# The low parts of a trunk kernel's projection weights: an accumulating transfer in place of VectorE's subtraction

## The chip, the core and the metric

The kernel runs on one core of one Trainium2 chip. The metric is the device time of one execution in microseconds (us). Before the change it is 2383.87 us, the median of three runs (2382.72 to 2384.26).

## What is computed

One inference step of a two-layer hybrid decoder trunk, for 1024 prompt tokens and 8 sample tokens that share all weights, model width 1024, everything in float32. Layer 0 mixes with a gated linear recurrence beside a convolution module, layer 1 with a short gated convolution; each layer ends in a SwiGLU with a hidden width of 2816.

```python
def _even_mixer(x, s0, conf_buf, w_in, w_out, ...):
    p = x @ w_in                                  # 1024 x 3072
    ...                                           # recurrence; depthwise convolution, LayerNorm, swish
    y = jnp.concatenate([o, c], axis=-1) @ w_out  # 1024 x 1024
def _odd_mixer(x, sc_buf, w_in, conv_w, w_out):
    p = x @ w_in                                  # 1024 x 3072
    ...
    return y @ w_out, ...
def _swiglu(x, w1, w3, w2):
    return (jax.nn.silu(x @ w1) * (x @ w3)) @ w2
def _trunk(...):
    for l in range(DEPTH):
        m, ... = _even_mixer(...) if l % 2 == 0 else _odd_mixer(...)
        x = _layernorm(ALPHA * x + m, ln_mix_w[l], ln_mix_b[l])
        x = _layernorm(ALPHA * x + _swiglu(x, ffn_w1[l], ffn_w3[l], ffn_w2[l]), ln_ffn_w[l], ln_ffn_b[l])
```

## The kernel before

The 1032 tokens stand in the columns and are cut into three chunks of 384, 384 and 264 (the last holds the 8 samples). Channels stand on the 128 partitions, in blocks of 128.

TensorE multiplies in a reduced-precision form of float32 (F32R). To keep float32's accuracy every operand is kept as two F32R tiles, a rounded high part and a low part that holds the rest, and every product is three matmuls: low weight by high activation (L141), high weight by low activation (L142), high by high (L143), all into one PSUM bank.

A *unit* is a block of weights for 128 outputs: 128 partitions by up to eight blocks of 128 inputs, 512 KB. `load_unit` (L123) makes one: it takes the tiles `wh` and `wl` (three buffers of each, `W_BUFS`) and `raw` (four buffers, `R_BUFS`), issues the load of `raw` on SyncE's queue (L131), and calls `split` (L119), in which ScalarE writes the high part (L120) and VectorE the low part (L121, `raw` minus `wh`). `mm` (L139) then runs 24 matmuls for a unit of eight input blocks and one chunk (12 for a unit of four). A buffer of `wh` and `wl` becomes free when the last matmul of its unit is done, so a unit can be prepared as soon as the unit three before it has been used up.

The *classic* projections are all that go through `load_unit`: the input and output projections of both mixers (`head_units`, `gate_units`, `conv_units`, `mix1`, `out_proj`), the upper SwiGLU products of the chunks that are not in the fast scheme (`ffn_up`), and the first two lower products of chunk 0 (`ffn_down`, units of four blocks). By the loops there are 281 such units in 282 loads (the first unit comes in two halves): 93 serve chunk 2 alone (20 and 36 in `Swiglu.main`, 6 and 6 in the heads of the two SwiGLUs, 8 and 8 in the output projections, 6 and 3 in `mix1`), 112 serve one chunk of 384, 41 two chunks, 19 three, and 16 are units of four blocks. The rest of the SwiGLU work has its own loads: `Swiglu.down` (load at L612) and `Swiglu.project` (a seven-product scheme over chunks 0 and 1, load at L677). They use the same buffers `wh`, `wl` and `raw`, and call `split` too. So do the activations.

Instructions are traced in program order, with priorities, and a scheduler fixes each engine's order at build time; every engine, and every queue, then runs in that order and waits for semaphores. GpSimd (POOL) has little to do: three transfers and two casts at the start, and the power of minus one half in `rsqrt_small` (L194), once in each of 15 normalisations and 16 times in the recurrence. In a normalisation TensorE broadcasts its result (L239).

Of the kernel before, what the change touches and what calls it, by code (L numbers as in the profile page):

```python
# [19 lines left out]
AF = mybir.ActivationFunctionType  # L20
ALU = mybir.AluOpType
# [47 lines left out]
def trunk(ctx: ExitStack, tc: tile.TileContext, xT, win0, wout0, win1, wout1, w1, w3, w2, vecs, sh, scf, ssc,  # L69
          masks, eye, yT, hp, cp_o, sp_o, hs, cs_o, ss_o):  # L70
    nc = tc.nc
    VE, SC, GP, PE = nc.vector, nc.scalar, nc.gpsimd, nc.tensor
# [46 lines left out]
    def split(hi, lo, src):  # L119
        SC.copy(hi, src)  # L120
        VE.tensor_tensor(lo, src, hi.bitcast(F32), ALU.subtract)  # L121

    def load_unit(src, kt, n=NK):  # L123

        wh = wsp.tile([P, NK, P], F32R, name="wh")
        wl = wsp.tile([P, NK, P], F32R, name="wl")
        raw = wsp.tile([P, NK * P], F32, name="raw", bufs=R_BUFS).rearrange("p (k f) -> p k f", f=P)
        src = src.rearrange("p (k f) -> p k f", f=P)
        for k in range(0, kt, n):
            e = min(k + n, kt)  # L130
            nc.sync.dma_start(raw[:, k:e], src[:, k:e])  # L131
            split(wh[:, k:e], wl[:, k:e], raw[:, k:e])
        return wh, wl, kt

    def mm(unit, c, parts=None):
# [16 lines left out]
    first_x = load_x(0, 2)  # L152
    next(first_x)
    first_unit = [load_unit(win0[4], NK, 4)]
    for _ in first_x:
        pass
# [111 lines left out]
    def out_proj(wsrc, chunks):  # L268

        for m in range(NK):  # L270
            u = load_unit(wsrc[m], NK)
            for c in chunks:
                residual(m, c, mm(u, c), True)

    def ffn_up(tile_of, l, m, chunks, put, table=True):

        sl = {}
        u = load_unit(w1[l, m], NK)
        for c in chunks:
            s = tile_of(CH[c][1] - CH[c][0])  # L280
            ps = mm(u, c)
            if table:
                SC.activation(s, ps, AF.Silu)
            else:
                SC.activation(s, ps, AF.Sigmoid)
                VE.tensor_tensor(s, ps, s, ALU.mult)
            sl[c] = s
        u = load_unit(w3[l, m], NK)
        for c in chunks:
            s = sl[c]  # L290
            VE.tensor_tensor(s, mm(u, c), s, ALU.mult)
            split(*put(m, c), s)
# [656 lines left out]
```

## Time and profile before

| | us |
|---|---|
| median of three runs | 2383.87 |
| the profiled execution | 2385.06 |
| its span, first to last instruction | 2383.2 |
| TensorE busy (matmuls) | 2333.2 |
| VectorE busy | 1701.4 |
| ScalarE busy | 874.2 |
| GpSimd busy | 45.3 |
| mean granted TensorE clock | 0.989 of full speed |

The profiled execution is 1.9 us longer than its span and 1.2 us longer than the median. Busy time counts an engine's own instructions, overlaps once; matmuls overlap each other, so one matmul's own duration is longer than the time by which it moves the next on. A wait is put down to what came last.

### The profile page before, as it was taken

What the parts mean: (1) busy time and instruction counts of PE and PEld (TensorE: products, weight loads), DVE (VectorE), ACT (ScalarE), POOL (GpSimd) and SP (SyncE); (2) the same over time, 40 slices, a digit from 0 to 9 for tenths busy, and PEclk for the clock granted to TensorE, in tenths of its full rate; (3) what the DMA queues carried; (4) which work ended last, traced back from release to release, by engine and by line L of the source; (5) the groups of instructions that cost most, each with busy time, mean ns of one, the idle gap of its engine ahead of it and who ended that gap; (6) DMA issues with size and microseconds to landing.
All of it is one profiled execution on the core that took longest, in us unless ns stands there. A gap on an engine that the chain in (4) does not pass through costs nothing.

```text
span 2383.2 us, 36586 instructions
## 1 busy us (share of the span) xinstructions
PE 2333.2 (98%) x14974; PEld 2293.0 (96%) x14974; DVE 1701.4 (71%) x2943; ACT 874.2 (37%) x1479; POOL 45.3 (2%) x40
## 2 busy tenths in 40 slices
PE   9999999999899999999998999999999999999997
PEld 8999899999899999999998999999999999999997
DVE  8998789897863336777686423667957777777775
ACT  5434353335631223332354211435513332332553
POOL 0000000000000000000000000000000000000000
PEclk9999999999999999999999999999999999999998
DMA  5322222453341221222342311334402222132663
GB/s 186 116 78 73 88 78 77 123 167 113 116 131 45 79 73 48 68 80 71 119 149 88 90 53 45 90 115 142 133 27 71 63 80 68 57 89 80 194 196 98
DMA packets 85560, 229.79 MB, mean 96 GB/s; under 512 B 8225, under 2 KB 26401, under 8 KB 85137
## 3 DMA queue, kind: packets, MB, share of 16 engines
q1 hardware_dynamic: 85232, 227.02, 30.9%
q8 instruction: 117, 1.92, 0.3%
q0 software_dynamic: 160, 0.45, 0.1%
q14 instruction: 51, 0.41, 0.1%
HBM read 220.22 MB, written 7.21 MB: 95 GB/s over the span
## 4 chain that ended last, share of the span: by engine, by line
PE 91%; DVE 4%; ACT 2%; POOL 1%; DMA 1%; issue 1%; SPq 0%; POOLq 0%; DVEq 0%; ACTq 0%
PE mm L141 23%; PE mm L142 23%; PE mm L143 23%; PE mm L692 6%; PE mm L693 6%; PE mm L691 6%; PE sm L335 2%; DVE wl L121 1%; POOL rs L194 1%; PE sm L239 1%; DVE r L216 1%; DVE acc L225 1%; ACT r L254 0%; PE sm L382 0%; ACT wh L120 0%
## 5 line engine op out<-in xcount | busy, mean ns | idle before, releaser
L120 ACT CAST wh<-raw 128x1024 fp32r<-128x1024 f32 (+1 forms) x466 | 468.6, 1007 | 899.4 <-PE mm L143 607.5
L121 DVE TENSOR_TENSOR wl<-raw,wh 128x1024 fp32r<-128x1024 f32 (+1 forms) x466 | 544.1, 1169 | 230.4 <-ACT wh L120 226.5
L141 PE MATMUL mm<-x2h,wl 128*128 128x264 f32 x1216 | 349.7, 288 | 7.0 <-DVE wl L121 6.9
L143 PE MATMUL mm<-x2h,wh 128*128 128x264 f32 x1216 | 346.8, 285 | 0.0
L142 PE MATMUL mm<-x2l,wh 128*128 128x264 f32 x1216 | 346.3, 285 | 0.0
L266 DVE TENSOR_TENSOR r<-r,mm 128x384 f32<-128x384 f32 (+1 forms) x336 | 171.5, 521 | 99.6 <-PE mm L143 99.2
L141 PEld LDWEIGHTS mm<-x2h,wl 128*128 128x128 f32 x1216 | 229.8, 189 | 9.6 <-DVE wl L121 8.3
L142 PEld LDWEIGHTS mm<-x2l,wh 128*128 128x128 f32 x1216 | 230.0, 189 | 1.6 <-issue 0.8
L143 PEld LDWEIGHTS mm<-x2h,wh 128*128 128x128 f32 x1216 | 229.1, 188 | 0.1
L141 PE MATMUL mm<-hb,wl 128*128 128x384 f32 (+1 forms) x672 | 211.4, 320 | 8.4 <-ACT hb L120 4.8
L142 PE MATMUL mm<-hb,wh 128*128 128x384 f32 (+1 forms) x672 | 213.1, 319 | 0.0
L143 PE MATMUL mm<-hb,wh 128*128 128x384 f32 (+1 forms) x672 | 212.8, 318 | 0.0
L482 DVE SCALAR_TENSOR_TENSOR cc<-r,vec,cc 128x256 f32<-128x256 f32 (+17 forms) x360 | 189.7, 561 | 0.9
L141 PEld LDWEIGHTS mm<-hb,wl 128*128 128x128 f32 x672 | 125.9, 190 | 10.7 <-ACT hb L120 7.0
L141 PE MATMUL mm<-x0ha,wl 128*128 128x384 f32 x384 | 132.7, 346 | 1.9 <-DVE wl L121 1.9
L143 PE MATMUL mm<-x0ha,wh 128*128 128x384 f32 x384 | 133.2, 347 | 0.0
L142 PE MATMUL mm<-x0la,wh 128*128 128x384 f32 x384 | 132.3, 345 | 0.8 <-DVE x0la L121 0.8
L143 PE MATMUL mm<-x0hb,wh 128*128 128x384 f32 x384 | 132.0, 344 | 0.0
L141 PE MATMUL mm<-x0hb,wl 128*128 128x384 f32 x384 | 131.3, 342 | 0.0
L142 PE MATMUL mm<-x0lb,wh 128*128 128x384 f32 x384 | 131.0, 341 | 0.0
L143 PE MATMUL mm<-x1hb,wh 128*128 128x384 f32 x384 | 130.8, 341 | 0.0
L142 PE MATMUL mm<-x1lb,wh 128*128 128x384 f32 x384 | 130.5, 340 | 0.0
(310 smaller groups left out, 5242.8 us busy)
## 6 DMA issues: line engine op xcount, KB each, us to landing
raw<-in_w SPq DMA_DIRECT2D x256, 512.0 KB, 3.7
raw<-in_win SPq DMA_DIRECT2D x88, 512.0 KB, 3.7
raw<-in_wout SPq DMA_DIRECT2D x48, 512.0 KB, 3.6
raw<-in_w SPq DMA_DIRECT2D x16, 256.0 KB, 2.7
out_yT<-r SPq DMA_DIRECT2D x8, 384.0 KB, 3.4
S0t<-in_sh SPq DMA_DIRECT2D x8, 256.0 KB, 3.2
out_hs<-S0t SPq DMA_DIRECT2D x8, 256.0 KB, 2.0
r<-in_xT SPq DMA_DIRECT2D x4, 384.0 KB, 7.5
```

The costliest lines, as they stand in the source:

```text
L120: SC.copy(hi, src)
L121: VE.tensor_tensor(lo, src, hi.bitcast(F32), ALU.subtract)
L141: PE.matmul(ps, wl[:, k, :], h, start=k == 0, stop=False)
L142: PE.matmul(ps, wh[:, k, :], l, start=False, stop=False)
L143: PE.matmul(ps, wh[:, k, :], h, start=False, stop=k == kt - 1)
L194: GP.tensor_tensor(dst, dst, mhalf[:p, :n], ALU.pow)
L266: VE.tensor_tensor(v, v, ps, ALU.add)
L335: PE.matmul(ps[:sr, c * 64:(c + 1) * 64].rearrange("p (b i) -> p b i", i=hh), kp[:, c * P:c * P + sr], qr, start=True, stop=True)
L482: VE.scalar_tensor_tensor(acc[:, lo:W], u[:, 30 + lo - d:30 + W - d], col(V_DW + (30 - d) * 4 + i), acc[:, lo:W], ALU.mult, ALU.add)
L691: PE.matmul(ps, w[1][:, k], t[0][:, k], start=k == 0, stop=False)
L692: PE.matmul(ps, w[0][:, k], t[1][:, k], start=False, stop=False)
L693: PE.matmul(ps, w[0][:, k], t[0][:, k], start=False, stop=k == 3)
```

## The change

`load_unit` calls a new function in place of `split`. ScalarE writes the high part as before. Then ScalarE, and no longer VectorE, writes the low tile, with the negated rounded weights. Then GpSimd's queue issues a transfer that reads the same weights from HBM a second time and adds them to what stands in the low tile. The result is the same low part, weights minus high part. `split` stays as it is for the activations, `Swiglu.down` and `Swiglu.project`.

```diff
+    def split_w(hi, lo, raw, src):
+
+        SC.copy(hi, raw)
+        SC.activation(lo, raw, AF.Copy, scale=-1.0)
+        nc.gpsimd.dma_start(lo, src, accum_op=ALU.add)
+
     def load_unit(src, kt, n=NK):
...
             nc.sync.dma_start(raw[:, k:e], src[:, k:e])
-            split(wh[:, k:e], wl[:, k:e], raw[:, k:e])
+            split_w(wh[:, k:e], wl[:, k:e], raw[:, k:e], src[:, k:e])
         return wh, wl, kt
```

## Rows read from the trace of the kernel before

**Rows 1.** The page's first part (busy us, share, instructions), busy tenths in 40 slices.

```profile
PE 2333.2 (98%) x14974; PEld 2293.0 (96%) x14974; DVE 1701.4 (71%) x2943; ACT 874.2 (37%) x1479; POOL 45.3 (2%) x40
...
PE   9999999999899999999998999999999999999997
...
DVE  8998789897863336777686423667957777777775
```

**Rows 2.** The page's chain that ended last, by engine.

```profile
PE 91%; DVE 4%; ACT 2%; POOL 1%; DMA 1%; issue 1%; SPq 0%; POOLq 0%; DVEq 0%; ACTq 0%
```

**Rows 3.** Waits, whole span: who waited for whom: us in total, times, longest.

```profile
ACT wh L120 <- PE mm L143: 607.5, 169, 10.4
...
PE sm L239 <- POOL rs L194: 15.6, 15, 2.1
...
PEld mm L141 <- DVE wl L121: 11.1, 9, 3.8
...
PE mm L141 <- DVE wl L121: 8.9, 7, 3.6
```

**Rows 4.** Instructions on tile raw: duration in ns min/median/max, first and last start.

```profile
L120 ACT CAST wh<-raw x466: 607/1050/1062, 7.3 to 2355.5; 128x1024 fp32r<-128x1024 f32 x140, 128x512 fp32r<-128x512 f32 x16
L121 DVE TENSOR_TENSOR wl<-raw,wh x466: 676/1219/1232, 8.1 to 2356.5; 128x1024 fp32r<-128x1024 f32 x140, 128x512 fp32r<-128x512 f32 x16
L131 SPq DMA_DIRECT2D raw<-in_w x144: 327/328/895, 283.1 to 2340.6; - x144
L131 SPq DMA_DIRECT2D raw<-in_win x90: 327/328/647, 1.2 to 1528.6; - x90
...
L131 SPq DMA_DIRECT2D raw<-in_wout x48: 327/328/340, 186.1 to 1653.9; - x48
```

**Rows 5.** ScalarE by line and shape: busy us, mean ns of one | idle before.

```profile
L120 ACT CAST hb<-hb 128x384 fp32r<-128x384 f32 x56 | 28.7, 512 | 30.5 <-DVE hb L733 30.5
...
L439 ACT ACTIVATE k<-mm 128x384 f32<-128x384 f32 x8 | 3.9, 487 | 0.0
```

**Rows 6.** Timeline of the last stage, three engines: start us, length us, instruction.

```profile
2311.43 1.05 ACT L120 CAST wh<-raw 128x1024 fp32r<-128x1024 f32 x1 [1.82 <-PE mm L143]
...
2312.51 1.23 DVE L121 TENSOR_TENSOR wl<-raw,wh 128x1024 fp32r<-128x1024 f32 x1 [0.65 <-ACT wh L120]
...
2311.24 0.28 PE L141 MATMUL mm<-x2h,wl 128*128 128x264 f32 x1
...
2317.04 0.28 PE L141 MATMUL mm<-x2h,wl 128*128 128x264 f32 x1
```

**Rows 7.** Stretches: their us, then busy us (and instructions) of each engine, clock, DMA.

```profile
2311.20:2331.70 20.50, 20.50 (x172) 20.50 (x171) 11.35 (x15) 9.11 (x13) 0.00 (x0) 1.00 0.58 180
...
1516.50:1537.00 20.50, 20.50 (x120) 20.50 (x119) 14.50 (x24) 12.00 (x24) 0.00 (x0) 1.00 0.38 122
505.00:520.20 15.20, 15.20 (x90) 15.20 (x89) 15.04 (x30) 5.17 (x9) 0.00 (x0) 1.00 0.55 151
1344.00:1513.00 169.00, 169.00 (x1081) 169.00 (x1080) 57.55 (x100) 26.89 (x61) 0.00 (x0) 1.00 0.18 51
```

**Rows 8.** The page's DMA issues: count, KB each, median us from issue to landing.

```profile
raw<-in_w SPq DMA_DIRECT2D x256, 512.0 KB, 3.7
...
raw<-in_w SPq DMA_DIRECT2D x16, 256.0 KB, 2.7
```

**Rows 9.** Timeline of GpSimd: the issue of its largest transfer.

```profile
2.50 0.54 POOL L164 DMA_DIRECT2D mraw<-in_masks  x1
```

**Rows 10.** DMA issues of the first 32 us: count, KB each, us to landing.

```profile
raw<-in_win SPq DMA_DIRECT2D x8, 512.0 KB, 5.9
...
mraw<-in_masks POOLq DMA_DIRECT2D x1, 256.0 KB, 7.2
```

**Rows 11.** The page's DMA queues: packets, MB, time as share of 16 engines' span.

```profile
q1 hardware_dynamic: 85232, 227.02, 30.9%
```

**Rows 12.** Waits of SyncE's queue: us in total, times, longest.

```profile
SPq L131 <- DVE wl L121: 1026.8, 204, 14.4
```

## The prediction

> **What bounds the kernel now.** Read the engines' busy times first: TensorE is busy for 98% of the span, VectorE for 71%, ScalarE for 37% [rows 1]. The chain that ended last says the same: 91% of it is TensorE's, 4% VectorE's [rows 2]. So VectorE's work, though long, is hidden nearly everywhere, even where its slices stand at 8 and 9 tenths (the first 650 us). What VectorE's subtraction costs now is read from the waits: TensorE's matmuls waited 8.9 us for it and its weight loads 11.1 us (two views of mostly the same waits) [rows 3]. That, some 10 to 20 us of 2383, is the most that taking the subtraction away can give directly.
>
> Next, who sets when a unit's low part is made. ScalarE's cast waited 607.5 us, 169 times, for a unit's last matmul [rows 3]: units are not late because ScalarE or VectorE is slow, they are started when one of three buffers comes free. It is a ring of three. The last stage shows one turn: a buffer comes free as a new unit begins at 2311.24, the cast starts at 2311.43, the subtraction runs from 2312.51 to 2313.74, and TensorE needs the unit at 2317.04, two units after the release [rows 6]. 3.3 us are spare. If a unit takes L from release to ready and is used for p, three buffers allow one unit per (L + p)/3, and TensorE is the bound only while L is below two units' time.
>
> The time of a unit is read from stretches in which TensorE never idles [rows 7]: 24 matmuls of 264 columns 2.9 us (20.50 x 24/172), of 384 columns 4.1 us (20.50 x 24/120), 12 of 384 columns 2.0 us (15.20 x 12/90), 72 for three chunks 11.3 us (169 x 72/1081). One such unit's last matmul ends about 0.15 us after the next has begun, so p is 3.05, 4.25 and 2.2.
>
> **What is removed.** 282 of the 466 subtractions, one for each load at L131 (144 + 90 + 48) [rows 4]. 266 are of 1.22 us and 16 units are half as wide, at 0.68: 335 us of VectorE's 1701, nearly all of it beside matmuls. I count back 9 us, the matmuls' own waits.
>
> **What is added on ScalarE.** 282 negations of the raw weights. The cast of the same tile takes 1.05 us, the half one 0.61 [rows 4]. An activation with a factor of -1 takes 0.487 us on 384 columns where the cast takes 0.512 [rows 5], so 1.05 us for 1024 columns, 0.62 for 512. 289 us together bring ScalarE to 1163 us, 49%: no bound, but inside every unit's L.
>
> **What is added on GpSimd and the DMA engines.** 282 accumulating transfers. Nothing in this trace accumulates, so I bound X, the time from the negation's end to the landing. Below, it is a plain 512 KB load from SyncE's queue, 3.7 us [rows 8], plus GpSimd's part of the issue, 0.54 us [rows 9]: 4.3, with a little sharing 4.5. Above, it is GpSimd's only large transfer, 256 KB in 7.2 us among the start's loads [rows 10], plus 1.0 us for twice the bytes (3.7 against 2.7 [rows 8]) and 0.8 for the reading of the sums: 9. What I take is built up: 227.02 MB held 16 engines for 30.9% of the span [rows 11], 736 us, or 1.7 us for 512 KB. To add, an engine must fetch the old content of the low tile too, a second pass over as many bytes: 1.7 more. And the transfer never runs alone. SyncE's next load waits for the buffer `raw` that the subtraction frees, 1026.8 us in 204 waits [rows 12]; now the negation frees it, so load and accumulation start at the same moment and share the engines; I charge a third of the load's 1.7. X = 3.7 + 0.5 + 1.7 + 0.6 = 6.5 us, nearer to the plain load than to the crowded start, as most of the kernel is not crowded. For a half-wide unit 2.7 + 0.5 + 0.85 + 0.3 = 4.35.
>
> The second pass rests on no row. The Trainium skill ("Collectives: The Full Stack", section "The bandwidth ceiling: the fold count and why AG ≠ RS ≠ AR") says that the DMA engines' adder needs two source reads for each piece, and that the reads halve the rate, not the adding. No run here shows it yet. Without that pass X would be 4.8 and the sum below about 50 us instead of 122.
>
> **The sum.** L is now the handover 0.1, cast 1.05, negation 1.05, handover 0.05, X 6.5: 8.75 us, where it was 2.4.
> - The 93 units of chunk 2 alone: (8.75 + 3.05)/3 = 3.93 against 2.9, so 1.03 each: 96 us. The bubble opens before each L141 that starts a unit.
> - The 16 half units: L = 0.1 + 0.62 + 0.62 + 0.05 + 4.35 = 5.74; (5.74 + 2.2)/3 = 2.65 against 2.0: 10 us.
> - The 112 units of one chunk of 384: (8.75 + 4.25)/3 = 4.33 against 4.1. That is 0.23 each, 26 us if all stood back to back, 0 if other matmuls (the recurrence, the norms) always lie between; I take 12.
> - The 60 units of two and three chunks last 7 us and more; two of them cover L wholly: 0.
> - The start: TensorE waits for the first half unit, whose subtraction takes 0.68 [rows 4]. In its place stand 0.62 and a transfer among the start's loads, 4.35 to 7.2: +5.
> - GpSimd's queue: the power of each normalisation (TensorE waits for it 15 times already, 15.6 us [rows 3]) now stands in order behind accumulations that wait for negations, which wait for TensorE to free a buffer. Behind one issue it costs 0.5 each, behind a whole unit 3: 8 to 45 us, I take 8.
> - SyncE's queue keeps its 282 loads in their order; each waits for ScalarE instead of VectorE, at nearly the same time, and there are four `raw` buffers: 0.
> 96 + 10 + 12 + 5 + 8 - 9 = 122 us on an execution of 2385.06, 2507; the median lies 1.2 lower: **2506 us**.
>
> With X = 4.5 the first term is 34 us ((6.75 + 3.05)/3 = 3.27), the second about 5, the third 0, the start 4, the queue 8, less 9: 42, or 2426. With X = 9 it is 174 (4.77 per unit), 25 for the half units, 70 of at most 119 for the third, 8, 8, less 9: 276, or 2660.
>
> **Rivals.**
> *The DMA engines become the bound.* A chunk-2 unit then needs 1.7 for the load and 3.4 for the accumulation, 5.1 us of all engines, more than its 2.9. In `Swiglu.main` one unit in three has no accumulation: (2 x 5.1 + 1.7) - 3 x 2.9 = 3.2 for each of 28 threes, 90 us; the other 37 units 2.2 each, 81; the wide ones up to 1.0 each, I take 80; start, queue and half units 13 more: 264 us, 2648. For it: the DMA share is 0.58 in the last stage already [rows 7]. Against: that share leaves room, and loads can run ahead.
>
> *The transfer is cheap and the kernel gets faster.* The point that decides is L = two units' time, 5.8 us for chunk 2: X = 3.5. Then no ring is late, the start costs 3, and TensorE gets back up to 20 us of waits and something of the norms, where VectorE's queue gets shorter: about 2370. At X = 3.7, the plain load's time, a chunk-2 unit loses 0.1 (9 us in all), start and queue take a few more, and gain and loss cancel: about 2383. Against: GpSimd's one transfer of half the size took 7.2 us, and a SyncE load of 512 KB beside it 5.9 [rows 10]. The Trainium skill ("DMA: Bandwidth & Descriptors", section "Anatomy of one DMA — SWDGE (gpsimd) path") gives a GpSimd transfer a fixed 2.0 us plus its bytes at 436 GB/s, 3.2 us for 512 KB as an estimate: by that rule this rival would come true. The row stands against it: the same rule gives 2.6 us for the 256 KB that took 7.2.
>
> *VectorE was the true bound of the first 650 us* (8 to 9 tenths busy), and its relief by 150 us there shows. Against: TensorE's own slices there stand at 8 and 9 tenths [rows 1], so at most its idle time returns, and that is in the 20 us above. That ScalarE becomes the bound is excluded by its 49%.
>
> **Chances.** The ring with X from 4.5 to about 8: 0.62. The DMA engines as bound, or a dearer transfer: 0.24, of which a little over half ends below 2670. The cheap transfer: 0.10, half of it faster, half the same. Slower than before but below 2420: 0.04. From 2420 to 2670 lie 0.62 + 0.14 = 0.76, near the 8 in 10 that are wanted. A measurement of this kernel tells 0.2%, some 5 us, from no change. Faster 0.05, the same 0.05, slower 0.90.
>
> **What would show it.** Landing times of the accumulations near 6.5 us, and longer than those of the plain loads. VectorE near 1366 us and ScalarE near 1163. TensorE waiting for the landing of `wl` before L141, most of it from 1150 to 1260 and after 2180 us, in bubbles of about 1 us once a unit; almost nothing from 692 to 1148 and 1344 to 1513 us, where units last 7 to 11 us. Stretches of chunk 2 alone going from 2.9 to about 3.9 us a unit. The forecast is wrong if the landings are under 4 us, if the bubbles stand at L239 behind GpSimd's power rather than at L141, or if the wide stages lose as well, which would be the engines' bandwidth.

## The result, and the profile after

The changed kernel takes 2653.34 us (2647.16 to 2659.31), the kernel before 2383.3: a ratio of 1.1133, interval 1.1104 to 1.1163. The forecast was 2506, so the loss is 270 us where 122 was forecast: the sign and the range held, the size did not. The profiled execution has a span of 2648.3 us.

The page of the changed kernel first: busy us of the engines, then the granted clock and the DMA engines' share in 40 slices.

```profile
PE 2411.4 (91%) x14974; PEld 2347.9 (89%) x14974; DVE 1405.6 (53%) x2661; ACT 1130.7 (43%) x1761; POOL 275.9 (10%) x322
...
PEclk8999999999899999999989999988899999999898
DMA  8764666897782551214855644978722221226895
```

Set against [rows 1]: TensorE was idle for 50.0 us (2383.2 - 2333.2) and is idle for 236.9, which is 187 more. And it is busy for 78 us longer with the same 14974 matmuls. 187 + 78 = 265, the whole difference of the spans. VectorE has lost 296 us and nobody gained by it.

What TensorE waits for, from the view of waits (who, for whom: us in total, times, longest):

```profile
POOL wl L127 <- ACT wl L126: 941.4, 181, 53.1
ACT wl L126 <- PE mm L147: 562.4, 208, 12.7
PE mm L147 <- DMA wl<-in_w: 110.0, 56, 10.5
...
PE mm L147 <- DMA wl<-in_wout: 49.5, 19, 10.2
PE mm L147 <- DMA wl<-in_win: 31.6, 14, 10.1
```

L147 is the L141 of before, L126 the negation, L127 the accumulation. The last three lines, 191 us in 89 waits, are the added idle time: TensorE waits for the accumulation to land. They are not the bubbles of about 1 us at each unit that the forecast had as a sign: 51 of the 89 are under 1.5 us, and 16 of over 3 us make 106 of the 191. The second line says why nobody starts it earlier: ScalarE's negation waits for a unit's last matmul with the low weights, as its cast did for the last of all in [rows 3].

The DMA issues (count, KB each, median us from issue to landing) and the two queues (packets, MB, time as a share of 16 engines' span):

```profile
raw<-in_w SPq DMA_DIRECT2D x256, 512.0 KB, 4.9
wl<-in_w POOLq DMA_DIRECT2D x128, 512.0 KB, 7.6
raw<-in_win SPq DMA_DIRECT2D x88, 512.0 KB, 6.5
wl<-in_win POOLq DMA_DIRECT2D x88, 512.0 KB, 7.1
...
wl<-in_wout POOLq DMA_DIRECT2D x48, 512.0 KB, 8.0
```
```profile
q0 software_dynamic: 40768, 143.59, 30.8%
q1 hardware_dynamic: 85232, 227.02, 25.9%
```

The accumulations land after 7.1 to 8.0 us, and the plain loads, 3.7 before [rows 8], now take 4.9 to 6.5. A MB that is added holds the engines for 0.308 x 2648.3 / 143.59 = 5.68 us, a MB on the queue of the loads, which carries the smaller transfers too, for 0.259 x 2648.3 / 227.02 = 3.02.

Where the time goes: stretches with the same work, first of the kernel after, then of the kernel before (stretch, its us, busy us and instructions of PE, PEld, DVE, ACT, POOL, then clock, DMA share, GB/s).

```profile
440.00:602.00 162.00, 146.34 (x883) 137.14 (x881) 95.07 (x218) 80.01 (x135) 33.30 (x39) 0.96 0.88 210
602.00:787.00 185.00, 146.73 (x866) 140.84 (x867) 84.95 (x145) 109.89 (x158) 32.74 (x37) 0.91 0.82 194
787.00:1259.00 472.00, 470.18 (x2906) 469.86 (x2906) 243.95 (x398) 138.00 (x190) 15.34 (x18) 1.00 0.34 89
1259.00:1397.00 138.00, 104.06 (x759) 100.04 (x758) 65.37 (x108) 78.36 (x110) 19.45 (x23) 0.89 0.73 183
...
1483.00:1652.00 169.00, 169.00 (x1080) 169.00 (x1079) 39.18 (x84) 39.82 (x75) 12.81 (x15) 1.00 0.43 99
1652.00:1927.00 275.00, 221.45 (x1276) 213.26 (x1275) 110.98 (x186) 153.02 (x215) 47.27 (x54) 0.90 0.82 192
...
2410.00:2648.00 238.00, 186.38 (x1365) 178.46 (x1363) 88.04 (x150) 116.45 (x153) 32.03 (x37) 0.91 0.76 199
```
```profile
414.00:554.00 140.00, 137.34 (x868) 131.76 (x867) 125.72 (x259) 50.20 (x95) 4.74 (x4) 0.99 0.44 136
554.00:697.00 143.00, 135.99 (x870) 133.49 (x869) 119.89 (x178) 79.30 (x126) 5.23 (x3) 0.98 0.41 126
697.00:1166.00 469.00, 467.93 (x2902) 467.61 (x2902) 265.94 (x417) 122.10 (x173) 0.00 (x0) 1.00 0.22 69
1166.00:1274.00 108.00, 97.61 (x763) 95.16 (x762) 85.63 (x126) 58.91 (x89) 3.91 (x2) 0.95 0.47 143
...
1343.00:1512.00 169.00, 169.00 (x1081) 169.00 (x1080) 58.06 (x101) 26.77 (x60) 0.00 (x0) 1.00 0.18 51
1512.00:1717.00 205.00, 201.34 (x1280) 198.79 (x1279) 156.82 (x225) 102.04 (x161) 4.92 (x3) 0.99 0.42 129
...
2199.00:2383.00 184.00, 169.38 (x1365) 166.17 (x1363) 126.65 (x184) 85.08 (x119) 4.76 (x3) 0.96 0.51 161
```

The stretches of long units lose 3 and 0 us. The last one loses 54, which the forecast had named. But 140 to 162, 143 to 185 and 205 to 275 us are stretches of single chunks of 384 columns for a large part, and the forecast had charged these units with 12 us in all. In the losing stretches the granted clock falls too, from 0.95 to 0.99 down to 0.89 to 0.96.

One turn of the ring shows both. It is from the timeline of 2446 to 2460 us (start us, length us, instruction, idle time before it), ScalarE and GpSimd:

```profile
2447.18 1.06 ACT L126 ACTIVATE wl<-raw 128x1024 fp32r<-128x1024 f32 x1 [1.21 <-PE mm L147]
2448.15 1.03 ACT L125 CAST wh<-raw 128x1024 fp32r<-128x1024 f32 x1
```
```profile
2448.53 0.88 POOL L127 DMA_DIRECT2D wl<-in_w  x1 [17.40 <-ACT wl L126]
```

The low buffer comes free at 2447.18, the negation ends at 2448.24, the transfer is issued at 2448.53, and the matmuls that need it begin at 2457.3, when it has landed. TensorE's last matmul of a unit had ended at 2453.2 and two of a normalisation at 2453.9; from then it was idle for 3.5 us. The negation runs ahead of the cast, here and in 236 of the 282 units, so the cast mostly no longer lies on the path. L, from free to landed, is 10.1 us here. The matmuls that follow, as stretches:

```profile
2457.30:2463.00 5.70, 5.66 (x26) 5.69 (x27) 2.84 (x4) 0.44 (x1) 0.00 (x0) 0.50 1.05 275
2463.00:2469.00 6.00, 6.00 (x48) 5.87 (x47) 2.42 (x4) 5.60 (x9) 1.71 (x2) 0.95 0.74 150
```

After these 3.5 us of waiting the granted clock is 0.50, the level of 1.2 GHz, and 26 matmuls take nearly as long as 48 do next. At the pace of the second stretch they would have taken 3.2 us: the wait costs its own 3.5 us and then 2.5 more behind it.

Matching every unit's first and last matmul in the two traces tells what each kind of unit lost (us; the number of units by this matching; the rest of a unit's loss lies between its ends):

| kind of unit | forecast | measured | of it idle ahead | of it slower matmuls |
|---|---|---|---|---|
| chunk 2 alone (88; the forecast counted 93) | 96 | 134 | 94 | 33 |
| one chunk of 384 (116; the forecast: 112) | 12 | 96 | 79 | 7 |
| half units (16) | 10 | 13 | 6 | 6 |
| two and three chunks (60) | 0 | 20 | 10 | 9 |
| the start | 5 | 10 | 8 | 1 |
| GpSimd's queue, waits given back | -1 | | | |
| units that VectorE still serves (184) | | -8 | 0 | -15 |

The matching sums to 197 us idle, 41 of slower matmuls and 27 between the ends; the page, which counts otherwise, has 187 idle and 78 more busy.

### The profile page after: what moved, and what is told of

Same layout as the page of the kernel before. It is cut to its first block, busy times and chain, and to the rows that moved or that the text cites. A ratio compares the mean times of both kernels' runs of the same rounds, so it can differ in the third digit from the quotient of the medians.

```text
span 2648.3 us, 37279 instructions
## 1 busy us (share of the span) xinstructions
PE 2411.4 (91%) x14974; PEld 2347.9 (89%) x14974; DVE 1405.6 (53%) x2661; ACT 1130.7 (43%) x1761; POOL 275.9 (10%) x322
## 3 DMA queue, kind: packets, MB, share of 16 engines
q0 software_dynamic: 40768, 143.59, 30.8%
q1 hardware_dynamic: 85232, 227.02, 25.9%
## 5 line engine op out<-in xcount | busy, mean ns | idle before, releaser
L126 ACT ACTIVATE wl<-raw 128x1024 fp32r<-128x1024 f32 (+1 forms) x282 | 290.6, 1031 | 563.0 <-PE mm L147 562.4
L147 PE MATMUL mm<-x2h,wl 128*128 128x264 f32 x1216 | 367.8, 303 | 118.8 <-DMA wl<-in_w 78.3
L147 PEld LDWEIGHTS mm<-x2h,wl 128*128 128x128 f32 x1216 | 243.7, 200 | 133.0 <-issue 48.4
L148 PE MATMUL mm<-x2l,wh 128*128 128x264 f32 x1216 | 360.8, 297 | 0.0
L127 POOL DMA_DIRECT2D wl<-in_w x144 | 123.3, 857 | 1482.0 <-DVE wl L121 730.2
L121 DVE TENSOR_TENSOR wl<-raw,wh 128x1024 fp32r<-128x1024 f32 (+1 forms) x184 | 209.6, 1140 | 94.4 <-ACT wh L120 92.0
L147 PE MATMUL mm<-hb,wl 128*128 128x384 f32 (+1 forms) x672 | 211.1, 319 | 3.8 <-ACT hb L120 3.6
L488 DVE SCALAR_TENSOR_TENSOR cc<-r,vec,cc 128x384 f32<-128x384 f32 (+15 forms) x360 | 191.2, 562 | 2.5
L147 PE MATMUL mm<-x1ha,wl 128*128 128x384 f32 x384 | 137.4, 358 | 44.7 <-DMA wl<-in_wout 22.6
L147 PE MATMUL mm<-x0ha,wl 128*128 128x384 f32 x384 | 135.1, 352 | 27.4 <-DMA wl<-in_win 13.1
L270 DVE SCALAR_TENSOR_TENSOR r<-r,mm 128x384 f32<-128x384 f32 (+1 forms) x96 | 48.9, 510 | 165.0 <-PE mm L149 164.6
L149 PE MATMUL mm<-x1ha,wh 128*128 128x384 f32 x384 | 135.5, 353 | 0.0
L148 PE MATMUL mm<-x1la,wh 128*128 128x384 f32 x384 | 134.7, 351 | 0.0
```

What stands on the lines that cost most here:

```text
L126: SC.activation(lo, raw, AF.Copy, scale=-1.0)
L127: nc.gpsimd.dma_start(lo, src, accum_op=ALU.add)
L147: PE.matmul(ps, wl[:, k, :], h, start=k == 0, stop=False)
L148: PE.matmul(ps, wh[:, k, :], l, start=False, stop=False)
L149: PE.matmul(ps, wh[:, k, :], h, start=False, stop=k == kt - 1)
L488: VE.scalar_tensor_tensor(acc[:, lo:W], u[:, 30 + lo - d:30 + W - d], col(V_DW + (30 - d) * 4 + i), acc[:, lo:W], ALU.mult, ALU.add)
```

## The experiments

The kernel each is made from, its edit, the expectation, the result. Ratios are to the kernel before, run beside it. L and the landings are medians from the traces. L is counted there from the start of ScalarE's first step for the low part (the negation; the cast in experiment 3) to the landing, so a late start of that step is not in it.

**1. What ScalarE's second pass costs alone.** From the kernel after; the addition on VectorE:

```diff
-        nc.gpsimd.dma_start(lo, src, accum_op=ALU.add)
+        VE.tensor_tensor(lo, raw, lo.bitcast(F32), ALU.add)
```


> As the changed kernel, but VectorE adds the weights to the negated high part; no accumulating transfer. ScalarE's negation and the new order of ScalarE's work stay. Ring theory (the loss is the transfer's time inside a ring of three buffers): the low part is ready about 2.4 to 3.5 us after a buffer comes free, under the 5.8 us that two chunk-2 units last, so the time is that of before, 2375 to 2395 us. Rival (ScalarE's 290 us more, or the order of work that the scheduler chose, cause the loss): over 2450 us.

2398.61 us, 1.0054 (1.0036 to 1.0073). ScalarE works 1130.2 us as in the kernel after, and the loss is 13 us by the ratio, 15 by the medians, a little more than expected. The transfer in the addition's place accounts for the other 255.

**2. What GpSimd's queue costs alone.** From the kernel before; the classic loads issued by GpSimd:

```diff
-            nc.sync.dma_start(raw[:, k:e], src[:, k:e])
+            nc.gpsimd.dma_start(raw[:, k:e], src[:, k:e])
```


> The kernel before, with the 282 plain loads of the classic units issued by GpSimd instead of SyncE; nothing is added. It shows what a plain transfer of 512 KB from GpSimd's queue costs from issue to landing. By the prediction's terms (3.7 us plain, 0.5 more for GpSimd's issue) 4.2 to 4.5 us, against 5.6 us for the fastest accumulations of the changed kernel: then the adding itself costs 1.1 to 1.4 us. Rival: the queue is what is dear, and the plain loads land after 5.5 us or more too. Time near before, 2383 to 2400 us, as loads run one buffer ahead.

2374.45 us, 0.9959 (0.9945 to 0.9972): a little faster than the kernel before, and the only version here that beats both. A transfer of the same size on the two queues, and GpSimd's queue, from its page:

```profile
q0 software_dynamic: 39616, 143.59, 19.8%
...
raw<-in_w POOLq DMA_DIRECT2D x128, 512.0 KB, 3.9
raw<-in_w SPq DMA_DIRECT2D x128, 512.0 KB, 3.7
```

So the queue is worth 0.2 us. The fastest accumulations of a whole unit in the kernel after landed 5.3 us from their issue (5.6 from the negation's end): adding costs 1.4 over the median of the plain transfers and 1.7 over the fastest plain ones of `in_win` and `in_wout` (3.6), where the forecast had put 1.7 for the second pass that it took on the Trainium skill's word ("Collectives: The Full Stack", section "The bandwidth ceiling: the fold count and why AG ≠ RS ≠ AR"). The queues agree in direction: the same 143.59 MB held the engines for 0.198 x 2371.3 / 143.59 = 3.27 us a MB when they were plain, and for 5.68 when they were added, 1.7 times as long (1.9 against the loads of the same run); the halved rate of that page would be 2.

**3. The wait without the bytes.** From the kernel before; after the subtraction, 32 bytes a partition of the low part go out and back, so that TensorE waits for a transfer but hardly anything is moved:

```diff
             split(wh[:, k:e], wl[:, k:e], raw[:, k:e])
+            t = wsp.tile([P, 8], F32, name="late", bufs=4)
+            low = wl[:, k, 0:8].bitcast(F32)
+            nc.sync.dma_start(t, low)
+            nc.gpsimd.dma_start(low, t)
```


> The kernel before (VectorE subtracts), and after each subtraction 32 bytes a partition of the low part go out to a small tile by SyncE's queue and come back by GpSimd's: the wait without the traffic; values stay. Ring theory: the low part is ready about 2.4 + 2 + 2.5 = 6.9 us after a buffer comes free; a chunk-2 unit then takes (6.9 + 3.05)/3 = 3.3 us in place of 2.9, 37 us for 93 units, and 0.3 for each of 16 half units: 2410 to 2440 us, more if the clock falls in the bubbles. Rival (bandwidth): 2383 to 2390 us.

2571.94 us, 1.0779 (1.0751 to 1.0806). From its page and its waits:

```profile
raw<-in_w SPq DMA_DIRECT2D x256, 512.0 KB, 3.8
...
late<-wl SPq DMA_DIRECT2D x282, 4.0 KB, 1.7
wl<-late POOLq DMA_DIRECT2D x282, 4.0 KB, 2.4
```
```profile
PE mm L145 <- DMA wl<-late: 109.7, 52, 11.1
```

The loads are at 3.8 us, so the engines are as free as before, and 189 us are lost all the same; of the 177 us by which this profiled execution is longer, 123 are idle and 54 are longer busy time of TensorE. L is 7.6 us. So a wait of 7.6 us with hardly any bytes costs 189 us, where 8.8 us with the bytes cost 270; and the expectation, worked out with the forecast's formula, was far too low again. The formula fails, not the wait.

**4. A deeper ring.** From the kernel after; four low buffers instead of three, and a control that gives up the same memory and keeps three. The memory comes from two other rings and from the area for GpSimd's descriptors (`dynamic_dma_scratch_size` 4096 to 2048); the last edit stands at all three places that make a low tile:

```diff
+L_BUFS = 4
...
-SL_BUFS = 6
+SL_BUFS = 4
...
-HB_BUFS = 18
+HB_BUFS = 17
...
-        wl = wsp.tile([P, NK, P], F32R, name="wl")
+        wl = wsp.tile([P, NK, P], F32R, name="wl", bufs=L_BUFS)
```


> Low parts get a ring of four buffers instead of three; the memory comes from six buffers elsewhere (sl 6 to 4, hb 18 to 17) and a smaller descriptor area, which e6_same_memory gives up too. Theory A (the wait that a unit has from its negation to its landing, carried by the ring of three): a unit's turn becomes about (1.05 + 1.05 + 7.9 + 3.05) / 4 = 3.3 us in place of 4.0 where chunk 2 runs alone, against the 2.9 of before, so some two thirds of the added idle time of TensorE (187 us) and of the time at a lower clock (78 us) come back: 2450 to 2520 us, at least 100 us under e6_same_memory. Theory B (the DMA engines are full: every weight is moved three times and the stretches are as long as the bytes need): a buffer more changes nothing, 2620 to 2670 us, within 30 us of e6_same_memory.

> Control for e5_four_low: the changed kernel with three low buffers and the same buffers given up elsewhere. Both theories: as the changed kernel, 2640 to 2680 us; anything above that is the price of the smaller rings elsewhere.

Four buffers: 2506.55 us, 1.0516 (1.049 to 1.0543). The control: 2658.42, 1.1154 (1.1134 to 1.1175). One buffer of 4 KB a partition gives back 152 us, with the same bytes and with accumulations that land later, not earlier, as these lines of the two pages say (four buffers, then the control). That is the ring. Under them two waits of the kernel with four:

```profile
wl<-in_w POOLq DMA_DIRECT2D x128, 512.0 KB, 8.7
```
```profile
wl<-in_w POOLq DMA_DIRECT2D x128, 512.0 KB, 7.7
```
```profile
PE mm L148 <- DMA wl<-in_w: 40.7, 36, 6.8
...
ACT wl L127 <- DMA raw<-in_w: 35.7, 22, 3.2
```

The first was 110.0 us, and the second is new: the negation now begins to wait for the loads. Late starts of the negation are left too: in 14 of the 44 waits of over 0.3 us for a landing, 53 of their 80 us, ScalarE began the negation right behind other work and not as its buffer came free.

A fifth buffer, and its control (`SL_BUFS` 2, `HB_BUFS` 14, the smaller descriptor area):

> The changed kernel with five low buffers; memory given up elsewhere: sl 6 to 2, hb 18 to 14, the smaller descriptor area. Set against e18_same_memory5. Theory A (waits carried by the ring): a turn of five, (10.3 + 1.05 + 2.9) / 5 = 2.9 us, is that of the shortest unit, so at least half of what e5_four_low still lost comes back: 60 us under e5_four_low plus what the smaller rings cost. Theory B (the rest is bytes): within 25 us of e5_four_low's 2507 us plus what the smaller rings cost.

> Control for e17_five_low: three low buffers, the same memory given up elsewhere. Both theories: the changed kernel plus what the smaller rings cost, 2655 to 2700 us.

2539.15 us, 1.0656 (1.0638 to 1.0673); the control 2649.85, 1.1113 (1.1075 to 1.115). Nothing more comes back, and 33 us of what four buffers gave are lost. The control loses nothing by the smaller rings; whether they cost something once the low ring is deep was not run. The expectation had forgotten what stands next in line:

```profile
ACT wl L127 <- DMA raw<-in_w: 120.9, 44, 7.0
...
ACT wl L127 <- DMA raw<-in_wout: 54.1, 23, 7.9
ACT wl L127 <- DMA raw<-in_win: 44.7, 21, 5.3
...
PE sm L238 <- DVE acc L235: 40.0, 8, 7.4
```

The first three are 220 us of waiting for raw weights, whose ring has four tiles and whose loads take 4.5 to 6.8 us (3.7 before). The last line shows how such a wait reaches TensorE: ScalarE runs in order, and while it stands at a negation for a load, the squares of a normalisation (L230) stand behind it. At 1284.3 us the negation began 3.1 us late for a load, the square followed at 1286.2, and TensorE went on at L238 at 1289.0, after 6.3 us idle. With four buffers this line has 3.3 us, in the control 6.5. TensorE's waits for landings are down to 52 us, so this run says that the low ring is no longer the limit; it doesn't say whether bytes are.

**5. Without the second reading of HBM.** From the kernel after; the addition reads the landed weights:

```diff
-        nc.gpsimd.dma_start(lo, src, accum_op=ALU.add)
+        nc.gpsimd.dma_start(lo, raw, accum_op=ALU.add)
```


> The accumulation reads the weights from the raw tile in SBUF, where they have landed, and no longer from HBM a second time. HBM traffic goes back to some 230 MB, the bytes that the DMA engines write and read in SBUF stay. Theory A (latency of the accumulating transfer as such): landings stay at 6.5 to 8 us and the time at 2600 to 2660 us. Theory B1 (the second read from HBM, colliding with the loads, makes the landing long): landings fall to about 5.6 us, the value without a load beside it, the loads go back to 3.7 us, and the time falls to 2480 to 2560 us.

2556.88 us, 1.0735 (1.0702 to 1.0769), 96 us less than the change, just inside the range of theory B1. The landing falls:

```profile
wl<-raw POOLq DMA_DIRECT2D x264, 512.0 KB, 5.8
```

and L from 8.8 to 7.0 us. Where the weights are read from costs 1.8 us of landing, and that returns 96 us: some 50 us for each us of L.

With four buffers as well:

> Both remedies: four low buffers as in e5_four_low and the weights added from the raw tile as in e3_from_raw. Theory A: with a wait of 7.0 us and a ring of four a turn is (7.0 + 1.05 + 3.05) / 4 = 2.8 us, just under the 2.9 us of the shortest unit, so that only the spread of the landings and the late starts on ScalarE are left: 2410 to 2460 us. If the two remedies don't add (the second one only moves the same wait): 2480 to 2510 us.

2506.71 us, 1.0507 (1.0491 to 1.0522). The two do not add, against theory A. The raw tile is now held until the sum has read it, and ScalarE's negations wait 133 us for loads (52 with four buffers alone). Of the 60 us that TensorE waited for landings in this trace some 20 follow a negation that began as its load landed, and some 30 one that began behind other work of ScalarE. The wait has moved, in part, to the raw ring.

**6. Which units.** From the kernel after; only units of two or three chunks get the transfer, or only those of chunk 2 alone; all others VectorE's subtraction. `chunks` is passed in from each caller, and the second kernel's condition is `tuple(chunks) == (2,)`:

```diff
-            split_w(wh[:, k:e], wl[:, k:e], raw[:, k:e], src[:, k:e])
+            if len(chunks) > 1:
+                split_w(wh[:, k:e], wl[:, k:e], raw[:, k:e], src[:, k:e])
+            else:
+                split(wh[:, k:e], wl[:, k:e], raw[:, k:e])
```


> Only units that serve two or three chunks get their low part by the accumulating transfer; the units of a single chunk keep VectorE's subtraction. Theory A: a unit of two chunks lasts 7 us or more on TensorE, so that a turn of (9 + 7) / 3 = 5.4 us fits under it: 2375 to 2400 us, no landing waited for by more than a few units. Theory B (bytes): these 60 units carry a fifth of the extra bytes, at stretches in which the engines were least used: 2380 to 2440 us. A theory in which ScalarE's second pass or GpSimd's queue costs something by itself: above 2400 us with the idle time before ScalarE's or GpSimd's successors.

> Only the units that serve chunk 2 alone (264 columns, 2.9 us on TensorE) get their low part by the accumulating transfer, all others by VectorE's subtraction. The complement of e7_wide_units as far as the shortest units go. Theory A (a unit's wait in the ring of three): these units lose most of what they lost in the changed kernel (134 us between the ends of their matmuls, 94 of it idle): 2460 to 2510 us, and the other units nothing. Theory B (the bytes, wherever they fall): a third of the accumulated bytes, spread over stretches whose engines were at half load or under: 2390 to 2440 us.

Wide units alone: 2415.29 us, 1.0127 (1.0101 to 1.0152), so the forecast's 0 for them was wrong by some 20 to 30 us; that lies above theory A's range and inside theory B's. Chunk 2 alone: 2541.21 us, 1.0652 (1.0619 to 1.0686), above the ranges of both theories. Matched unit by unit, the units of chunk 2 lose 138 us there and 134 in the whole change, though a third of the bytes is moved: what they lose is their own. If the parts add up, 2653 - 2383 - 33 - 156 leaves some 80 us for the units of one chunk and the half units.

**7. Two cures that cure little.** Each accumulation cut in two halves, so that matmuls may start at the first; and the negation on VectorE, because 22 of the 88 waits over 0.3 us that I found in the change (101 of their 192 us) follow a negation that began over 1 us after its buffer was free, ScalarE being at the normalisation of the next chunk:

```diff
-        nc.gpsimd.dma_start(lo, src, accum_op=ALU.add)
+        n = max(lo.shape[1] // 2, 1)
+        for k in range(0, lo.shape[1], n):
+            nc.gpsimd.dma_start(lo[:, k:k + n], src[:, k:k + n], accum_op=ALU.add)
```
```diff
-        SC.activation(lo, raw, AF.Copy, scale=-1.0)
+        VE.tensor_scalar(lo, raw, -1.0, None, ALU.mult)
```


> The changed kernel with each accumulation cut in two transfers of four row blocks each, so that the matmuls of the first four can begin at the first half's landing. Same bytes, twice the issues on GpSimd (0.86 us each). Theory A: the wait to the first half falls from 7.6 towards the 5.5 us that a transfer of 256 KB took in the changed kernel, so a turn falls by some 0.5 us: 2540 to 2610 us. Theory B (bytes): 2640 to 2680 us. If GpSimd's issuing is what delays: above 2653 us.

> The changed kernel with the negation on VectorE in place of ScalarE; the transfer as before. In the changed kernel 22 of the 88 waits of TensorE for a landing, 101 of their 192 us, follow a negation that began 1 to 8 us after its buffer was free, because ScalarE was still at the normalisation of the next chunk. Theory C (these late starts are a cause of their own): 50 to 100 us come back, 2550 to 2600 us. Theory D (VectorE is as late as ScalarE, or the late starts don't decide): 2630 to 2680 us.

Halves: 2597.85 us, 1.0897 (1.0872 to 1.0922), 55 less, as the wait theory had it. VectorE: 2643.17 us, 1.1086 (1.1057 to 1.1115), 10 less, which the overlapping intervals do not tell from no change: VectorE is late as often (21 late starts ahead of 93 us of waiting). Late starts precede half of the waiting on either engine; moving the negation does not cure them, and what they cost by themselves was not isolated.

**8. The bytes without the wait.** From the kernel before; the same weights added into spare HBM that nobody reads, VectorE's subtraction kept. It is not the change's transfer exactly: the sum goes to HBM, and the last two kernels read it from the raw tile. Five kernels; the edit of the last two, of which the second has five raw tiles (and the memory of experiment 4's control):

```diff
             split(wh[:, k:e], wl[:, k:e], raw[:, k:e])
+            d = spare[len(used) % 16]
+            used.append(0)
+            nc.gpsimd.tensor_copy(raw[:, k, 0:1], wl[:, k, 0:1].bitcast(F32))
+            nc.gpsimd.dma_start(d[:, k:e], raw[:, k:e], accum_op=ALU.add, max_dma_last_dim=4096)
```


> The kernel before (VectorE subtracts), and beside each classic load GpSimd issues an accumulating transfer of the same weights into a spare region of HBM that nobody reads: the traffic without the wait. Rival (the DMA engines' bandwidth is the bound): most of the loss comes back, 2500 us or more. Ring theory: loads land later but are one buffer ahead, so TensorE waits little: 2385 to 2430 us.

> The kernel before, with VectorE's subtraction, and beside it the same accumulation of each unit's weights, into spare HBM that nobody reads, issued by GpSimd only once that unit's subtraction has been done (a transfer of 32 bytes a partition out of the low part stands ahead of it on the same queue). It is e4_traffic_only with the bytes moved when the changed kernel moves them. Theory A (a unit's wait): TensorE waits for no accumulation, the loads get longer by the shared engines, which their four buffers hide for the most part: 2385 to 2440 us. Theory B (bytes): 2600 us or more, as the changed kernel.

> e10_paced_traffic again, now with an order that holds: the 32 bytes a partition out of the low part are written into the very region that the accumulation then adds to, so that each accumulation waits for its own unit's subtraction (in e10_paced_traffic GpSimd issued all of them in the first 870 us, with the DMA engines busy throughout). Theory A (a unit's wait in the ring): TensorE waits for none of these transfers, the loads get longer and their four buffers hide most of that: 2385 to 2440 us. Theory B (the bytes): 2600 us or more. Between 2440 and 2600 us the bytes count by themselves too, through the loads and the transfers of the scan.

> Side traffic at the right time, without a landing that anything but a buffer waits for: the kernel before, VectorE's subtraction kept; after each subtraction GpSimd writes one column of the raw tile from the low part (so that the next step can't be issued earlier) and then adds the raw tile into spare HBM. The raw tile is held until that transfer has read it, as in e3_from_raw. Not the changed kernel's bytes exactly: the sum goes to HBM and not to SBUF. To be set against e3_from_raw (2557 us), which moves the same weights from the same tile at the same time and has TensorE wait for them. Theory A (a unit's wait in the ring of three low buffers): the raw ring of four alone carries the wait, as in e12_four_low_raw, where it was behind some 24 us: 2390 to 2450 us. Theory B (the bytes, and the engines they occupy): 2540 us or more.

> e15_paced_raw with five raw tiles in place of four (the memory given up elsewhere is that of e6_same_memory, which cost some 5 us). In e15_paced_raw a raw tile is held from the load's issue to the end of the side transfer, some 4.3 + 3 + 7.5 us, so that a turn of four is 3.7 us against 2.9 us of the shortest units. Theory A (waits carried by rings): with five a turn is 3.0 us, 2410 to 2480 us. Theory B (the engines are full where these units run, their bytes alone take longer than 2.9 us a unit): no change, 2540 to 2580 us.

The first adds from HBM with nothing ahead of the issue, the second with a small copy out of the low part ahead of it. Neither tells: 2669.51 us, 1.1196, and 2666.31, 1.118, but GpSimd issued all additions in the first 870 us, ahead of their units. The stretches of the first one:

```profile
0.00:870.00 870.00, 634.12 (x3663) 599.97 (x3664) 520.63 (x1132) 252.60 (x544) 253.31 (x311) 0.83 1.04 239
870.00:2665.00 1795.00, 1759.65 (x11312) 1748.47 (x11311) 1185.24 (x1812) 619.46 (x936) 18.00 (x11) 0.99 0.30 92
```

All its loss is in the first stretch, with the engines full. The third writes that copy into the region that is added to, which holds the order but brings waits of its own: 2714.37 us, 1.1373; VectorE waited 143 us for the copy, and TensorE 103 us for GpSimd's power in the normalisations (15.6 before). The fourth orders them by a column that GpSimd writes: 2572.7 us, 1.0797 (1.0752 to 1.0843), 189 us with no low part that anyone waits for. But the raw ring carries a wait there. With five raw tiles it is 2491.76 us, 1.0452 (1.0413 to 1.0491), 81 us less. ScalarE's waits for loads, first with four tiles, then with five:

```profile
ACT wh L120 <- DMA raw<-in_w: 189.2, 51, 8.7
ACT wh L120 <- DMA raw<-in_wout: 68.6, 22, 7.8
ACT wh L120 <- DMA raw<-in_win: 40.0, 13, 6.2
```
```profile
ACT wh L120 <- DMA raw<-in_w: 88.9, 31, 6.8
ACT wh L120 <- DMA raw<-in_wout: 60.0, 18, 8.6
ACT wh L120 <- DMA raw<-in_win: 16.4, 7, 4.7
```

In the kernel before these waits are 0.4 us. So bytes alone, with no wait in the low ring, still cost 108 us with five raw tiles, between the two theories' figures; part of it is again a ring's wait (165 us of ScalarE's waiting), and which part stays open.

## Why the prediction was right in sign and wrong in size

*The bound and the ring: right.* TensorE waits for the landing ahead of the first matmul of a unit, ScalarE for TensorE to free a buffer, and a fourth low buffer takes back 152 of 270 us (experiment 4), while a wait with hardly any bytes brings 189 (experiment 3).

*X and L: right by two errors.* X was put at 6.5 us and is 7.9 for a whole unit (quartiles 6.9 and 9.0), most likely because load and addition share the engines more than the 0.6 charged for it: the fastest, 5.6, lie under the 5.9 of the other three terms, but the sharing was not isolated. But the negation was put behind the cast, and in 236 of 282 units it runs ahead of it, so 1.05 us fall out of L. L was 8.75 in the forecast and has a median of 9.0 for whole units, 8.8 for all, counted from the negation's start. That the sum of L came out was luck.

*From L to time: the step that failed.* With the L that the run shows, the formula would still have given about 98 us for chunk 2 and at most 37 for the units of one chunk. They lost 134 and 96. Four things were left out.
- The start of the negation. The sum has 0.1 us between the release of a buffer and ScalarE. In the run 101 of 192 us of waiting follow a negation that began over 1 us late (experiment 7). Counted as negations that ScalarE began right behind other work, late starts precede 43 of the 59 us of waiting at the first low matmul of units that begin with chunk 0 or 1 (the start left out), and 54 of the 116 us at those that begin with chunk 2. So that the 94 idle us of chunk 2 come near the formula's 98 is no proof of the formula.
- The term of the units of one chunk, 12 us, was taken as a part of a margin of 0.23 us a unit between a turn and a unit's time. A margin that small is no cover when L scatters: a quarter of these units has L over 10.0, and a short turn gives nothing back, since TensorE can't use a unit faster than 4.1 us. Each unit's own L put in the formula (p taken as 4.1) gives 44 us where their median, 9.0, gives 30, and the late starts come on top.
- The clock. No term priced it. By the traces' granted clock TensorE was busy for 156 us at 0.50, against 39 in the kernel before; half of the 117 more, some 58 us as an estimate, is what the clock made of the 78 us of longer busy time. What the other 20 are was not traced. The row of before on which a unit's time rests stands at 1.00 [rows 7]; after a wait of some us it is 0.50. p in the formula grows with the wait that the formula gives. In the mean over all 1216 matmuls of one kind it reads:

```profile
L147 PE MATMUL mm<-x2h,wl 128*128 128x264 f32 x1216 | 367.8, 303 | 118.8 <-DMA wl<-in_w 78.3
```

  303 ns against 288 in the same row of the kernel before, and 118.8 us of waiting where there were 7.0.
- The units of two and three chunks, 0 in the forecast, lost 20, half of it in slower matmuls (the table), and 33 where they alone get the transfer (experiment 6). That two of them cover L holds inside their stretches, which lose 0 to 3 us, and not for all 60; at which of the others it fails was not traced.

*The small terms.* The start cost 10 instead of 5. GpSimd's queue cost nothing: TensorE's waits for the power went from 15.6 to 5.4 us, although the issue of an accumulation holds GpSimd for 0.855 us. VectorE 1405.6 and ScalarE 1130.7 us stand near the 1366 and 1163 forecast.

*Where it would show.* The last stage (54 us) and 1259 to 1397 us (30) lose, the long units don't, as forecast. That most of it would lie there was wrong: from 440 to 787 us 64 are lost and from 1652 to 1927 another 70.

*The rivals.* The cheap transfer fell: 3.9 us is the price of a plain one on GpSimd's queue, and adding costs 1.4 more at the least. The rule of the Trainium skill ("DMA: Bandwidth & Descriptors", section "Anatomy of one DMA — SWDGE (gpsimd) path"), 3.2 us for 512 KB as an estimate, lies under both. VectorE as the true bound fell: its 296 us came back nowhere. The DMA engines as the bound had 2648 us, very near the result, but a time that fits is no proof: with them as the bound a fourth low buffer could not have given 152 us at the same bytes. They count in a second way, by making L longer (8.8 us, and 7.0 without the second reading of HBM: 270 and 174 us), and, through the longer loads, in the raw ring, for which ScalarE waits with four and five buffers. How the last 125 us, with four buffers, divide between full engines, the raw ring and late starts is not settled.

## What to carry to other kernels

When work moves from an engine to a transfer, its price is not the engine time but the time from free buffer to landing, divided by the depth of the ring, and it begins only when the engine ahead of the transfer is free; compare it with the shortest unit, and count a margin of a few tenths of a us as none. Add what the waits cost afterwards: the matmuls behind a wait of several us ran at half the clock here, and that made some 58 us beside 187 idle. If the transfer must be, a deeper ring gave back 152 us here, a nearer source 96, halves 55; the first two together gave no more than the first alone.

## What the runs showed of the hardware that was not expected

- An accumulating transfer of 512 KB into SBUF held the engines 5.68 us per MB where the same transfers, plain on the same queue, held them 3.27. It landed 5.3 us after its issue at the least (5.6 after the negation), and 7.9 after the negation in the median, 12.2 at most.
- Its issue holds GpSimd longer than a plain one's, 855 ns against 528 for the same tile (the plain one in experiment 2):

```profile
L127 POOL DMA_DIRECT2D wl<-in_w x144: 847/855/907, 343.0 to 2614.4; - x144
```

- 4 KB out and back cost 1.7 and 2.4 us in transfers, and that alone was worth 189 us.
- The granted clock was 0.50 for 5.7 us after TensorE had waited 3.5 us, with the DMA engines at 1.05 in that stretch.
